# Two empty tiles of 32 and 128 bytes that move SBUF addresses in a float32 decoder-layer kernel

## The chip, the core and the metric

The kernel runs on one core of one Trainium2 chip. The metric is the device time of one execution in microseconds: the median of three executions, 1381.23 us before the change (1381.03 to 1384.09). One further execution was recorded by the hardware profiler; it took 1381.79 us, of which 1380.0 us lie between the first and the last instruction.

## The reference: what is computed

One inference step of a single hybrid layer, for two request groups that share the weights: a prompt of 256 tokens and 8 sample requests of 4 tokens, 288 token columns in all. All tensors are float32. Cut to what matters:

```
h    = rmsnorm(x) * (1 + sc1) + sh1                 # adaLN: sh, sc, g = silu(c) @ w_ada + b_ada
proj = h @ w_in                                     # 2048 -> 4632 columns
mix  = concat[pool_mixer(u), ssd_mixer(z, xbc, dt)] @ w_out
x    = x + g1 * mix
h2   = rmsnorm(x) * (1 + sc2) + sh2
gate, val = split(h2 @ w_up)                        # 2048 -> 2 * 5504
x    = x + g2 * ((silu(causal_dwconv(gate)) * val) @ w_down)
y    = rmsnorm(x)
```

The outputs are y for both groups and the new pooling, convolution, SSM and FFN states.

## The kernel before, in words

Features lie on the 128 partitions and tokens on the free axis, so each activation is a list of tiles of 128 x 288 float32, 1,152 bytes on a partition. Weights come from memory as one stream of pieces of 128 x 1024 float32 (`load`, into tiles `raw`), in the order in which they are used.

Every product of weights and features is made of three TensorE matmuls (`mm3`, lines 247 to 252). Both operands are split into a rounded high part and a remainder in the fp32r format, and the small-times-small product is left out. ScalarE writes the high part of a weight piece (`whi`, line 238), VectorE the remainder (`wlo`, line 240). The high and low parts of the features are the tiles `h1h`/`h1l`, `mixh`/`mixl`, `h2h`/`h2l` (made by `new_operand`) and `ah`/`al`. In a product the weights are the operand that is loaded into the array (LDWEIGHTS, 128 columns) and the features are the operand that streams past them (288 columns):

```
        nc.tensor.matmul(ps, whi[:, w], bh, start=first, stop=False)   # L250
        nc.tensor.matmul(ps, whi[:, w], bl, start=False, stop=False)   # L251
        nc.tensor.matmul(ps, wlo[:, w], bh, start=False, stop=last)    # L252
```

The stages follow each other: `xbc` and `mm_dt` (first input projection, with the adaLN products `adag` between), `mm_uz` (the rest of the input projection, with the SSD mixer between), `mm_out`, `mm_up`, then `mm_gate` and `mm_val` in turn for each of 40 column tiles of the FFN, with `mm_down` in three blocks. A projection of 16 feature tiles is 48 of these matmuls.

Where things lie in SBUF is set by pools. Pool `kp` lives through the kernel and grows from the low addresses; `mx`, `w0` and `sx` lie above it in the first half, and `ff` and `w2` take their place in the second half. Pool `w1` lies at the high end, from the right, and does not depend on the others. There are two sets of split weight slots: the two `whi` and two `wlo` slots of `w1`, used from the start, and two and two more in `w2`, added at line 1062 when `mm_out` has reached its sixth tile (m = 5). From then on pieces take the four slots in turn, so that in the FFN each `mm_gate` projection (two pieces) reads the slots of `w2`, each `mm_val` projection those of `w1`, and `mm_down` half from each. Counted over the program, 5,400 of the 8,736 matmuls of `mm3` read slots of `w1` and 3,336 read slots of `w2`.

A scheduler orders the instructions from their dependencies; the early part is kept in the order written.

Of the kernel before, what the change touches and what calls it, by code (L numbers as in the profile page):

```python
# [11 lines left out]
F32 = mybir.dt.float32  # L12
# [5 lines left out]
P = 128  # L18
# [119 lines left out]
def kernel(ctx: ExitStack, tc, ins, outs):  # L138
# [4 lines left out]
    kp = ctx.enter_context(tc.tile_pool(name="kp", bufs=1))  # L143
    pm = ctx.enter_context(tc.tile_pool(name="pm", bufs=3, space=PSUM))
    px = ctx.enter_context(tc.tile_pool(name="px", bufs=4, space=PSUM))
    pa = ctx.enter_context(tc.tile_pool(name="pa", bufs=1, space=PSUM))

    def aux(name):
        return px.tile([P, 512], F32, tag="aux", name=name)
# [49 lines left out]
    def new_operand(name):  # L199
        xhi[0] = [kp.tile([P, N], F32R, tag="xhi", name=f"{name}h{k}", bufs=KT) for k in range(KT)]  # L200
        xlo[0] = [kp.tile([P, N], F32R, tag="xlo", name=f"{name}l{k}", bufs=KT) for k in range(KT)]
# [263 lines left out]
    ups = mx.tile([P, 4, NB, 19], F32, name="ups")  # L465
    nc.vector.memset(upp[:, :, 0:15], 0.0)

    new_operand("h1")

    selr = mx.tile([P, 32], F32R, name="selr")  # L470
# [541 lines left out]
    mx_ctx.close()  # L1012
    ff = ctx.enter_context(tc.tile_pool(name="ff", bufs=1, reuse_waits="tile"))
    w2 = ctx.enter_context(tc.tile_pool(name="w2", bufs=1, reuse_waits="tile"))
    x = ff.tile([P, KT, N], F32, name="x")


# [340 lines left out]
```

## Time and profile before

| | |
|---|---|
| median of three executions | 1381.23 us |
| profiled execution | 1381.79 us, span 1380.0 us |
| TensorE matmuls (PE) | 99% of the span, 10,569 instructions |
| TensorE weight loads (PEld) | 91% |
| VectorE (DVE) | 60% |
| ScalarE (ACT) | 41% |
| GpSimd (POOL) | 16% |
| DMA queue of the weight stream | 62.5% of 16 engines |

In the views, PE rows are matmuls and PEld rows are weight loads, which run beside the matmul before them. A matmul's listed duration holds its latency and overlaps the next one, so the pace of TensorE is read from the distance between the starts of neighbouring matmuls and not from the listed duration. Names stand as out<-in by the program's tiles.

### The profile page before, as it was taken

The numbers are of one execution on the slowest core, as the hardware profiler recorded it, in microseconds if no ns is written. First come the engines' busy times: TensorE is split into PE (matmuls) and PEld (weight loads), VectorE is DVE, ScalarE is ACT, GpSimd is POOL, SyncE is SP. The second block draws the span as 40 slices with busy tenths as digits, with TensorE's granted clock in tenths as the row PEclk, the third lists the DMA queues.
The fourth block names the chain that finished last, engine by engine and source line by source line (L and its number), as shares of the span: only waits on it lengthen the run. The fifth ranks groups of instructions, "written<-read, shape, count | busy, mean of one in ns | idle before, by whom it ended". The sixth has DMA issues, their size and how long they took to land.

```text
span 1380.0 us, 26263 instructions
## 1 busy us (share of the span) xinstructions
PE 1360.7 (99%) x10569; PEld 1260.0 (91%) x10569; DVE 822.8 (60%) x1376; ACT 570.1 (41%) x889; POOL 224.4 (16%) x430
## 2 busy tenths in 40 slices
PE   8999999999999999999999999999999999999997
PEld 7888987776779899989999999999999999999997
DVE  5776557877574448654655445656565555566553
ACT  4223233478553335533433333443433334443452
POOL 0000001212122213111221001212120012122221
PEclk9999999999999999999999999999999999999998
DMA  9987756888887868687555455555554555555531
GB/s 380 408 355 296 281 215 258 328 297 297 306 338 294 317 244 284 231 278 290 189 176 181 171 167 185 202 184 184 187 172 162 184 196 180 195 190 190 185 119 70
DMA packets 97194, 323.20 MB, mean 234 GB/s; under 512 B 10736, under 2 KB 19888, under 8 KB 97072
## 3 DMA queue, kind: packets, MB, share of 16 engines
q1 hardware_dynamic: 93168, 310.63, 62.5%
q0 software_dynamic: 3184, 9.69, 1.8%
q8 instruction: 83, 1.36, 0.4%
q10 hardware_dynamic: 720, 1.19, 0.2%
q14 instruction: 39, 0.32, 0.1%
HBM read 309.78 MB, written 10.39 MB: 232 GB/s over the span
## 4 chain that ended last, share of the span: by engine, by line
PE 94%; DVE 4%; ACT 1%; issue 1%; POOL 0%; DMA 0%; DVEq 0%; POOLq 0%; ACTq 0%
PE mm_down L250 7%; PE mm_down L252 7%; PE mm_down L251 7%; PE mm_gate L250 6%; PE mm_val L251 6%; PE mm_val L252 6%; PE mm_val L250 6%; PE mm_gate L252 6%; PE mm_gate L251 6%; PE adap L279 4%; PE xbc L252 4%; PE xbc L250 4%; PE xbc L251 4%; PE mm_out L250 3%; PE mm_out L251 3%; PE mm_out L252 2%
## 5 line engine op out<-in xcount | busy, mean ns | idle before, releaser
L250 PE MATMUL mm_down<-ah,whi_down 128*128 128x288 f32 x688 | 203.8, 296 | 0.0
L252 PE MATMUL mm_down<-ah,wlo_down 128*128 128x288 f32 x688 | 203.6, 296 | 0.0
L251 PE MATMUL mm_down<-al,whi_down 128*128 128x288 f32 x688 | 203.4, 296 | 0.0
L251 PE MATMUL mm_val<-h2l,whi_val 128*128 128x288 f32 x640 | 191.3, 299 | 0.0
L252 PE MATMUL mm_val<-h2h,wlo_val 128*128 128x288 f32 x640 | 190.0, 297 | 0.0
L250 PE MATMUL mm_gate<-h2h,whi_gate 128*128 128x288 f32 x640 | 189.9, 297 | 0.0
L250 PE MATMUL mm_val<-h2h,whi_val 128*128 128x288 f32 x640 | 189.0, 295 | 0.0
L251 PE MATMUL mm_gate<-h2l,whi_gate 128*128 128x288 f32 x640 | 188.9, 295 | 0.0
L252 PE MATMUL mm_gate<-h2h,wlo_gate 128*128 128x288 f32 x640 | 188.7, 295 | 0.0
L240 DVE TENSOR_TENSOR wlo_gate<-raw_gate,whi_gate 128x1024 fp32r<-128x1024 f32 x80 | 97.9, 1225 | 138.6 <-ACT whi_gate L238 136.5
L240 DVE TENSOR_TENSOR wlo_down<-raw_down,whi_down 128x1024 fp32r<-128x1024 f32 x96 | 108.2, 1127 | 116.7 <-ACT whi_down L238 115.9
L238 ACT CAST whi_down<-raw_down 128x1024 fp32r<-128x1024 f32 x96 | 92.2, 960 | 169.2 <-PE mm_down L251 122.0
L238 ACT CAST whi_gate<-raw_gate 128x1024 fp32r<-128x1024 f32 x80 | 83.8, 1050 | 162.8 <-PE mm_gate L251 70.5
L250 PE MATMUL xbc<-h1h,whi_xbc 128*128 128x288 f32 x448 | 136.3, 306 | 1.7 <-ACT cvp L593 0.9
L238 ACT CAST whi_val<-raw_val 128x1024 fp32r<-128x1024 f32 x80 | 84.0, 1050 | 128.1 <-issue 102.2
L252 PE MATMUL xbc<-h1h,wlo_xbc 128*128 128x288 f32 x448 | 132.1, 302 | 2.6 <-DVE wlo_xbc L240 2.5
L251 PE MATMUL xbc<-h1l,whi_xbc 128*128 128x288 f32 x448 | 132.8, 297 | 0.0
L251 PEld LDWEIGHTS mm_down<-al,whi_down 128*128 128x128 f32 x688 | 129.8, 189 | 0.0
L252 PEld LDWEIGHTS mm_down<-ah,wlo_down 128*128 128x128 f32 x688 | 129.7, 189 | 0.0
L250 PEld LDWEIGHTS mm_down<-ah,whi_down 128*128 128x128 f32 x688 | 129.7, 188 | 0.0
L250 PEld LDWEIGHTS mm_gate<-h2h,whi_gate 128*128 128x128 f32 x640 | 120.1, 188 | 5.0 <-ACT ah L1123 3.4
L250 PEld LDWEIGHTS mm_val<-h2h,whi_val 128*128 128x128 f32 x640 | 120.9, 189 | 0.0
(322 smaller groups left out, 2992.9 us busy)
## 6 DMA issues: line engine op xcount, KB each, us to landing
raw_adap<-wflat SPq DMA_DIRECT2D x128, 512.0 KB, 5.5
raw_gate<-wflat SPq DMA_DIRECT2D x80, 512.0 KB, 3.5
raw_val<-wflat SPq DMA_DIRECT2D x80, 512.0 KB, 3.5
raw_ada<-wflat SPq DMA_DIRECT2D x64, 512.0 KB, 9.4
raw_xbc<-wflat SPq DMA_DIRECT2D x55, 512.0 KB, 7.2
raw_down<-wflat SPq DMA_DIRECT2D x48, 512.0 KB, 3.5
raw_out<-wflat SPq DMA_DIRECT2D x32, 512.0 KB, 6.9
raw_down<-wflat SPq DMA_DIRECT2D x32, 384.0 KB, 2.9
```

The costliest lines, as they stand in the source:

```text
L238: yield nc.scalar.copy(hi[:, :n], raw[:, a:a + n])
L240: nc.vector.tensor_tensor(lo[:, :n], raw[:, a:a + n], hi[:, :n].bitcast(F32), ALU.subtract)
L250: nc.tensor.matmul(ps, whi[:, w], bh, start=first, stop=False)
L251: nc.tensor.matmul(ps, whi[:, w], bl, start=False, stop=False)
L252: nc.tensor.matmul(ps, wlo[:, w], bh, start=False, stop=last)
L279: nc.tensor.matmul(ps[32 * j:32 * j + 32, :nb], sc_c[:, k, :], raw[:, c:c + nb], start=(k == 0), stop=(k == KT - 1), tile_position=(0, 32 ...
```

## The change

Two tiles that nothing writes or reads are allocated: one of 32 bytes on each partition in `kp`, just ahead of the first call of `new_operand`, and one of 128 bytes at the bottom of `w2`.

```
+    def shift(pool, nbytes):
+        pool.tile([P, nbytes // 4], F32, name="shift")
...
     nc.vector.memset(upp[:, :, 0:15], 0.0)
+    shift(kp, 32)
     new_operand("h1")
...
     w2 = ctx.enter_context(tc.tile_pool(name="w2", bufs=1, reuse_waits="tile"))
+    shift(w2, 128)
     x = ff.tile([P, KT, N], F32, name="x")
```

On all engines and in the DMA queues the built program has the same instructions in the same order with the same waits as before. What differs is addresses. Everything that is allocated in `kp` after the first tile, and all of `mx`, `w0`, `sx` and `ff`, lies 32 bytes higher; the tiles of `w2` lie 160 bytes higher (32 + 128); `w1` stays. Byte addresses on a partition:

| tiles | before | now | remainder by 128 before | now |
|---|---|---|---|---|
| `h1h`, `mixh`, `h2h` (16 tiles, 1,152 apart) | 22,656 and on | 22,688 and on | 0 | 32 |
| `h1l`, `mixl`, `h2l` | 41,088 and on | 41,120 and on | 0 | 32 |
| `ah` (17 tiles) | 108,032 and on | 108,064 and on | 0 | 32 |
| `al` (17 tiles) | 127,616 and on | 127,648 and on | 0 | 32 |
| `whi` slots of `w2` | 147,200 and 151,296 | 147,360 and 151,456 | 0 | 32 |
| `wlo` slots of `w2` | 155,392 and 159,488 | 155,552 and 159,648 | 0 | 32 |
| `raw` slot of `w2` | 163,584 | 163,744 | 0 | 32 |
| `whi` slots of `w1` | 212,960 and 217,056 | the same | 96 | 96 |
| `wlo` slots of `w1` | 221,152 and 225,248 | the same | 96 | 96 |

Inside a slot the weights of one matmul lie 512 bytes after those of the one before. Feature tiles that are used one after the other are 1,152 bytes apart, which is 128 more or less by a remainder of 256, so their remainder by 256 changes by 128 from one feature tile to the next.

More of the change, by code (lines that the diff above doesn't have):

```diff
@@ L146, with shift @@
     pa = ctx.enter_context(tc.tile_pool(name="pa", bufs=1, space=PSUM))
+    def shift(pool, nbytes):
+        pool.tile([P, nbytes // 4], F32, name="shift")
     def aux(name):
@@ L466 @@
     nc.vector.memset(upp[:, :, 0:15], 0.0)
+    shift(kp, 32)
     new_operand("h1")
@@ L1014 @@
     w2 = ctx.enter_context(tc.tile_pool(name="w2", bufs=1, reuse_waits="tile"))
+    shift(w2, 128)
     x = ff.tile([P, KT, N], F32, name="x")
```

## The prediction

> **What bounds the kernel now.** I read the page's busy shares, then the chain of waits, then busy times by stage, then single matmuls.
>
> ```profile
> span 1380.0 us, 26263 instructions
> PE 1360.7 (99%) x10569; PEld 1260.0 (91%) x10569; DVE 822.8 (60%) x1376; ACT 570.1 (41%) x889; POOL 224.4 (16%) x430
> PE 94%; DVE 4%; ACT 1%; issue 1%; POOL 0%; DMA 0%; DVEq 0%; POOLq 0%; ACTq 0%
> ```
>
> ```profile
> core 0: us, PE busy (x) PEld busy (x) DVE busy (x) ACT busy (x) POOL busy (x), PEclk, DMA share, GB/s
> 0.00:200.00 200.00, 193.55 (x1792) 169.68 (x1793) 128.10 (x240) 63.94 (x89) 5.96 (x16) 1.00 0.86 331
> 200.00:400.00 200.00, 196.68 (x1512) 144.56 (x1510) 149.49 (x312) 122.62 (x247) 41.02 (x68) 0.99 0.78 289
> 650.00:1366.00 716.00, 716.00 (x5363) 716.00 (x5362) 403.06 (x587) 283.25 (x400) 125.63 (x253) 1.00 0.52 176
> ```
>
> The chain that ended last is 94% TensorE. From 650 to 1366 us nothing makes TensorE wait: 716.00 of 716.00 us busy, DMA at half load, clock granted in full. There 5,363 matmuls take 716 us, 133.5 ns apart on average, nearly all of them 128x288 products. The time of this stage is therefore a number of matmuls times a pace, and only the pace can move it. The first 400 us have 9.8 us of TensorE idle time, so a faster pace is worth a little less there.
>
> **Does the pace depend on where the operands lie?** The change alters no instruction, so this is the question. The trace holds a natural comparison: mm_gate and mm_val have the same shapes and the same feature tiles, in turns, in one stage. They differ in the set of weight slots: mm_gate reads w2, whose slots lie at remainder 0 by 128 like the feature tiles; mm_val reads w1, at remainder 96.
>
> ```profile
> L251 PE MATMUL mm_val<-h2l,whi_val 128*128 128x288 f32 x640 | 191.3, 299 | 0.0
> L252 PE MATMUL mm_val<-h2h,wlo_val 128*128 128x288 f32 x640 | 190.0, 297 | 0.0
> L250 PE MATMUL mm_val<-h2h,whi_val 128*128 128x288 f32 x640 | 189.0, 295 | 0.0
> L250 PE MATMUL mm_gate<-h2h,whi_gate 128*128 128x288 f32 x640 | 189.9, 297 | 0.0
> L251 PE MATMUL mm_gate<-h2l,whi_gate 128*128 128x288 f32 x640 | 188.9, 295 | 0.0
> L252 PE MATMUL mm_gate<-h2h,wlo_gate 128*128 128x288 f32 x640 | 188.7, 295 | 0.0
> ```
>
> The three lines of mm_val list 299, 297 and 295 ns, those of mm_gate 297, 295 and 295. The starts of three projections in a row, 48 matmuls each, say it as pace:
>
> ```profile
> 914.28 0.29 PE L250 MATMUL mm_gate<-h2h,whi_gate 128*128 128x288 f32 x1
> ...
> 920.67 0.29 PE L250 MATMUL mm_val<-h2h,whi_val 128*128 128x288 f32 x1
> ...
> 927.10 0.29 PE L250 MATMUL mm_gate<-h2h,whi_gate 128*128 128x288 f32 x1
> ```
>
> mm_gate takes 6.39 us, which is 133.1 ns a matmul; mm_val takes 6.43 us, 134.0 ns. The difference is 0.04 us in 48, or 0.83 ns a matmul. Inside mm_val it is not even:
>
> ```profile
> 912.05 0.30 PE L251 MATMUL mm_val<-h2l,whi_val 128*128 128x288 f32 x1
> ...
> 912.45 0.30 PE L251 MATMUL mm_val<-h2l,whi_val 128*128 128x288 f32 x1
> ...
> 912.86 0.30 PE L251 MATMUL mm_val<-h2l,whi_val 128*128 128x288 f32 x1
> ...
> 913.26 0.30 PE L251 MATMUL mm_val<-h2l,whi_val 128*128 128x288 f32 x1
> ```
>
> One feature tile (three matmuls) takes 0.40 us, the next 0.41, the next 0.40. The feature tiles alternate by 128 in their remainder by 256 while the slots do not, so I read this as: weight reads and feature reads get in each other's way by a few ns, depending on the distance of their addresses. No wait is listed at these matmuls. This reading is an inference; nothing in the trace shows a memory bank.
>
> **The change, part by part.**
>
> *The 32 bytes, for the w1 products (5,400 of 8,736).* Features go from remainder 0 to 32 by 128 and the w1 slots stay at 96. The distance from features to weights goes from 96 or 224 by 256 (the fast and the slow half above) to 64 or 192. No matmul of before has that distance with ordinary weights, so I bound it from both sides. The nearest row for a gain that stays within one stage is mm_gate: if w1 products run at the w2 pace, 5,400 x 0.83 ns = 4.5 us are won, of which the 1,344 xbc products (1.1 us) lie in the first 200 us and are partly lost in waits: 3.4 to 4.5 us. A farther row has the very distance that comes: cse streams csr, which lies at byte 127,520, remainder 32 by 128, while either one repeated column or the w1 weights of mm_uz are loaded.
>
> ```profile
> 275.84 0.43 PE L740 MATMUL cse<-csr,selr 128*128 128x288 f32 x2
> 276.10 0.29 PE L250 MATMUL mm_uz<-h1h,whi_uz 128*128 128x288 f32 x1
> ...
> 277.70 0.43 PE L740 MATMUL cse<-csr,selr 128*128 128x288 f32 x2
> 277.96 0.29 PE L250 MATMUL mm_uz<-h1h,whi_uz 128*128 128x288 f32 x1
> ```
>
> Two matmuls take 0.26 us from start to start, 130 ns each with 5 ns of rounding; I use 131. Against 134.0 that is 3.0 ns, and 5,400 x 3.0 = 16 us. This is the far end for a gain, because those matmuls stand alone among others and load one repeated column half the time. They also say that a feature operand at an odd multiple of 32 bytes costs nothing by itself. The end for a loss is the slow feature tile of mm_val, 0.41 / 3 = 136.7 ns, in every w1 product: 2.7 ns x 5,400 = +14.6 us. Between -16 and +14.6 I take a little more than the nearest row, **-5 us**: the slow half has a distance that goes away, and the one sample of the new distance is fast.
>
> *The 128 bytes, for the w2 products (3,336).* Features and w2 slots both move to remainder 32 by 128, so their distance stays 0 or 128 by 256. With 160 bytes for one and 32 for the other, the feature tiles that had the one distance get the other. Each half of the tiles has either, so I take **0**; the bound is the spread between slot sets, 0.83 ns x 3,336 = 2.8 us either way.
>
> *Other engines and the DMAs.* They read and write moved tiles as well. Splitting shows no price of place, at w1 (val) or w2 (gate):
>
> ```profile
> L238 ACT CAST whi_val<-raw_val 128x1024 fp32r<-128x1024 f32 x80 | 84.0, 1050 | 128.1 <-issue 102.2
> L238 ACT CAST whi_gate<-raw_gate 128x1024 fp32r<-128x1024 f32 x80 | 83.8, 1050 | 162.8 <-PE mm_gate L251 70.5
> L240 DVE TENSOR_TENSOR wlo_gate<-raw_gate,whi_gate 128x1024 fp32r<-128x1024 f32 x80 | 97.9, 1225 | 138.6 <-ACT whi_gate L238 136.5
> raw_gate<-wflat SPq DMA_DIRECT2D x80, 512.0 KB, 3.5
> raw_val<-wflat SPq DMA_DIRECT2D x80, 512.0 KB, 3.5
> ```
>
> ScalarE takes 1050 ns for both. VectorE and ScalarE wait for work (136.5 us on ScalarE's result, 70.5 us for a free slot), and loads land in 3.5 us where a projection lasts 6.4, so even 1% on each would stay hidden behind TensorE after 400 us. I take **0**. If that cover were gone, in the first 200 us at 0.86 DMA share, 1% of slower loads would be at most 2 us.
>
> *Sum.* -5 + 0 + 0 on the profiled 1381.8 us gives 1376.8; the profiled execution lies 0.6 us above the median shown, so on the median's scale it is **1376.2 us**, -0.36%. What a measurement of this kernel tells from no change is about 0.3%, or 4.1 us: 0.77 ns on each w1 product. The forecast stands just beyond that.
>
> **The rivals.**
>
> *The place doesn't matter enough: 1381 us.* The alternation averages out: the new distances 64 and 192 are again one fast and one slow half. For it: distances 0 and 128 (mm_gate) and 96 and 224 (mm_val) differ by only 0.83 ns on average. Against it: the slow half exists at all. A rule speaks for this rival. The Trainium skill, "TensorE: Matmul & The Clock Gate", Part 2, says that TensorE has two independent SBUF read ports and that loading the next weights takes no read bandwidth from the running matmul. "SBUF — State Buffer", Door 1, gives lines of 16 bytes, of which 32 and 128 are whole multiples. By both the time would stay at 1381; the 0.40 and 0.41 us in turn do not agree with a full independence.
>
> *The new distance is the bad one: slower.* The mechanism is the one above at the same place, the 5,400 w1 products: both 64 and 192 lie in the slow state that mm_val has on every other feature tile. Fully locked it costs +14.6 us, 1396; half of it, +7, gives 1388. It decides the sign from 0.77 ns a product on. For it: only one of the four known distances is clearly slow, and nothing says how wide that region is. Against it: cse at 131.
>
> *A deep gain: 1365 us.* All w1 products run at the pace of cse, -16 us. For it: the same row. Against: cse never runs in a long row with full weights.
>
> **How the numbers follow.** Forecast (mild gain, its own range 1371 to 1379) 0.42, of which 0.10 lies within 0.3%; deep gain 0.12; no change 0.25; slower 0.21. So faster 0.44, same 0.35, slower 0.21. The range reaches down to 1364, just past the deep gain, and up to 1391, the slow rival's middle and some more; beyond it lies the fully locked case, about 0.1, and some 0.05 below.
>
> **What would show it.** Between 650 and 1366 us the same 5,363 matmuls should take some 3 us less, with PE still busy throughout. A mm_val projection should fall from 6.43 to 6.39 us or below, without the turn of 0.40 and 0.41; a mm_gate projection should stay at 6.39. ACT 1050 ns and DVE 1225 ns should not move. I am wrong in size if mm_val drops under 6.35 or if mm_gate moves as well; wrong in sign if mm_val rises to 6.5; wrong in mechanism if the time moves and the pace of these two does not, or if it is the first 400 us that move.

## The result, and the profile after

The changed kernel takes 1374.32 us (median of five executions, 1373.55 to 1375.51) where the kernel before took 1381.23 us in the same comparison: a ratio of 0.9948 with a 95% interval of 0.9933 to 0.9962, or 6.9 us less. The profiled execution took 1375.51 us with a span of 1373.7 us, 6.3 us under the 1380.0 us of before. One execution below, the profiled one of e4, ran at a granted clock of 0.751 and took 1635 us, where the other five of that kernel have 0.995 to 0.997; it is left out of e4's median and ratio.

The page of the changed kernel, its busy shares and its chain of waits:

```profile
span 1373.7 us, 26263 instructions
PE 1353.4 (99%) x10569; PEld 1252.7 (91%) x10569; DVE 822.1 (60%) x1376; ACT 569.9 (41%) x889; POOL 224.9 (16%) x430
PE 94%; DVE 4%; DMA 1%; issue 0%; ACT 0%; POOL 0%; SPq 0%; DVEq 0%; POOLq 0%; ACTq 0%
```

TensorE is busy 7.3 us less, the other engines do what they did, and the chain is TensorE's as before. Where the time went is seen when both executions are cut at the same instructions: the start of mm_out, of mm_up, of the first mm_gate, and the last mm_down. First the kernel before, then the changed one; the columns are the stretch, its length, busy time and number of instructions of each engine, the clock, the DMA share and GB/s.

```profile
0.00:391.50 391.50, 383.68 (x3269) 310.69 (x3269) 269.13 (x529) 181.60 (x326) 45.79 (x82) 1.00 0.82 310
391.50:522.50 131.00, 129.05 (x954) 110.96 (x950) 62.08 (x108) 46.12 (x66) 26.79 (x41) 1.00 0.80 303
522.50:561.00 38.50, 38.50 (x291) 38.38 (x289) 32.63 (x58) 21.08 (x37) 12.15 (x19) 1.00 0.77 268
561.00:1366.60 805.60, 805.60 (x6035) 796.57 (x6034) 452.03 (x665) 320.07 (x458) 139.63 (x289) 1.00 0.54 186
```

```profile
0.00:390.60 390.60, 381.77 (x3269) 308.75 (x3269) 269.06 (x529) 181.50 (x326) 45.85 (x82) 1.00 0.82 310
390.60:520.90 130.30, 128.31 (x954) 110.18 (x950) 62.08 (x108) 46.21 (x66) 26.98 (x41) 1.00 0.81 305
520.90:559.30 38.40, 38.40 (x291) 38.30 (x289) 32.49 (x58) 20.99 (x37) 12.16 (x19) 1.00 0.77 261
559.30:1360.30 801.00, 801.00 (x6035) 791.99 (x6034) 451.60 (x665) 319.95 (x458) 139.88 (x289) 1.00 0.56 187
```

Each stretch has the same number of matmuls in both. The FFN gives 4.6 us (805.60 to 801.00, TensorE busy throughout), the first 390 us 0.9, mm_out 0.7, mm_up 0.1. In the first stretch TensorE is busy 1.9 us less and the stretch is only 0.9 us shorter: half of the gain there is lost in waits.

The groups of mm_gate and mm_val in the changed kernel, whose lines are numbered 5 higher:

```profile
L255 PE MATMUL mm_gate<-h2h,whi_gate 128*128 128x288 f32 x640 | 190.0, 297 | 0.0
L256 PE MATMUL mm_gate<-h2l,whi_gate 128*128 128x288 f32 x640 | 189.1, 295 | 0.0
L256 PE MATMUL mm_val<-h2l,whi_val 128*128 128x288 f32 x640 | 189.0, 295 | 0.0
L257 PE MATMUL mm_val<-h2h,wlo_val 128*128 128x288 f32 x640 | 188.8, 295 | 0.0
L257 PE MATMUL mm_gate<-h2h,wlo_gate 128*128 128x288 f32 x640 | 188.4, 294 | 0.0
L255 PE MATMUL mm_val<-h2h,whi_val 128*128 128x288 f32 x640 | 188.2, 294 | 0.0
```

mm_val went from 295, 299 and 297 ns to 294, 295 and 295; mm_gate stayed. The starts of the same three projections that the prediction shows (the 20th of the 40 pairs of mm_gate and mm_val, and the mm_gate behind it), and of three feature tiles inside mm_val, in the changed kernel:

```profile
910.35 0.29 PE L255 MATMUL mm_gate<-h2h,whi_gate 128*128 128x288 f32 x1
...
916.74 0.29 PE L255 MATMUL mm_val<-h2h,whi_val 128*128 128x288 f32 x1
...
923.09 0.29 PE L255 MATMUL mm_gate<-h2h,whi_gate 128*128 128x288 f32 x1
```

```profile
919.92 0.29 PE L255 MATMUL mm_val<-h2h,whi_val 128*128 128x288 f32 x1
...
920.31 0.29 PE L255 MATMUL mm_val<-h2h,whi_val 128*128 128x288 f32 x1
...
920.71 0.29 PE L255 MATMUL mm_val<-h2h,whi_val 128*128 128x288 f32 x1
```

mm_gate takes 6.39 us as before, mm_val 6.35 instead of 6.43. The turn of 0.40 and 0.41 us is gone, and what is left is 0.39 and 0.40. Averaged over the 40 mm_val projections, a feature tile of the slow half takes 396.2 ns after 405.3, and one of the fast half 397.7 after 399.2: most of the gain comes from the slow half, and the fast half gained a little too. Averaged over all w1 products that follow each other directly, the three matmuls of a feature tile take 396.9 ns after 401.0; those of w2 take 399.0 after 399.2.

### The profile page after: what moved, and what is told of

Read it like the earlier page. It is cut to its first block, busy times and chain, and to the rows that moved or that the text cites. A ratio compares the mean times of both kernels' runs of the same rounds, so it can differ in the third digit from the quotient of the medians.

```text
span 1373.7 us, 26263 instructions
## 1 busy us (share of the span) xinstructions
PE 1353.4 (99%) x10569; PEld 1252.7 (91%) x10569; DVE 822.1 (60%) x1376; ACT 569.9 (41%) x889; POOL 224.9 (16%) x430
## 4 chain that ended last, share of the span: by engine, by line
PE 94%; DVE 4%; DMA 1%; issue 0%; ACT 0%; POOL 0%; SPq 0%; DVEq 0%; POOLq 0%; ACTq 0%
PE mm_down L255 7%; PE mm_down L256 7%; PE mm_down L257 7%; PE mm_gate L255 6%; PE mm_val L256 6%; PE mm_gate L257 6%; PE mm_gate L256 6%; PE mm_val L257 6%; PE mm_val L255 6%; PE adap L284 4%; PE xbc L257 4%; PE xbc L255 4%; PE xbc L256 4%; PE mm_out L255 3%; PE mm_out L256 3%; PE mm_out L257 2%
## 5 line engine op out<-in xcount | busy, mean ns | idle before, releaser
L243 ACT CAST whi_gate<-raw_gate 128x1024 fp32r<-128x1024 f32 x80 | 83.7, 1048 | 161.9 <-PE mm_gate L256 70.5
L243 ACT CAST whi_val<-raw_val 128x1024 fp32r<-128x1024 f32 x80 | 84.1, 1051 | 125.0 <-issue 100.1
L256 PE MATMUL xbc<-h1l,whi_xbc 128*128 128x288 f32 x448 | 132.2, 296 | 0.0
```

The costliest lines, as they stand in the source:

```text
L243: yield nc.scalar.copy(hi[:, :n], raw[:, a:a + n])
```

## The experiments

The theory under test: the pace of a product follows the distance, by 256, from the streamed features to the weights that are being loaded beside them. The rivals: the features' own place, the slots' own place, or something else than the weight stream. Three starts, those of the 20th mm_gate, its mm_val and the next mm_gate, give the pace in each run. All runs, with the ratio to the kernel before in the same comparison and its interval:

| run | distances w1 | w2 | mm_gate us | mm_val us | time us | ratio |
|---|---|---|---|---|---|---|
| before | 96, 224 | 0, 128 | 6.39 | 6.43 | 1381.2 | |
| the change | 64, 192 | 0, 128 | 6.39 | 6.35 | 1374.3 | 0.9948 [0.9933, 0.9962] |
| e1 32 bytes alone | 64, 192 | 0, 128 | 6.39 | 6.35 | 1376.1 | 0.9960 [0.9947, 0.9974] |
| e2 128 bytes alone | 96, 224 | 0, 128 | 6.38 | 6.40 | 1379.3 | 0.9985 [0.9976, 0.9995] |
| e3 w1 slots 32 lower | 64, 192 | 0, 128 | 6.40 | 6.35 | 1373.9 | 0.9953 [0.9939, 0.9967] |
| e4 32 and 64 bytes | 64, 192 | 64, 192 | | | 1372.4 | 0.9937 [0.9925, 0.9949] |
| e5 64 bytes in kp | 32, 160 | 0, 128 | 6.40 | 6.35 | 1376.4 | 0.9966 [0.9952, 0.9979] |
| e6 96 bytes in kp | 0, 128 | 0, 128 | 6.40 | 6.39 | 1376.7 | 0.9967 [0.9956, 0.9978] |
| e7 distance restored | 96, 224 | 0, 128 | 6.39 | 6.42 | 1380.9 | 1.0002 [0.9993, 1.0011] |
| e8 as e4 | 64, 192 | 64, 192 | 6.34 | 6.35 | 1371.2 | 0.9932 [0.9918, 0.9945] |
| e9 one column, old places | | | 6.33 | 6.35 | 1372.1 | 0.9934 [0.9918, 0.9951] |
| e10 one column, new places | | | 6.33 | 6.35 | 1370.6 | 0.9922 [0.9907, 0.9937] |
| e11 96 bytes, low parts 128 on | 0, 128 | 0, 128 | 6.39 | 6.41 | 1374.1 | 0.9947 [0.9932, 0.9962] |
| e12 as e8, low parts 128 on | 64, 192 | 64, 192 | 6.35 | 6.35 | 1372.8 | 0.9935 [0.9920, 0.9949] |

The intervals are wide beside the differences: by time alone e1, e5 and e6 cannot be told from each other. The paces in the traces tell them apart.

### e1: the 32 bytes alone

```
+    shift(kp, 32)
     new_operand("h1")
```

> The 32-byte tile alone. Distance theory (the pace of a product follows the distance, by 256, from the streamed features to the weights being loaded): w1 products have the changed kernel's distances 64 and 192, so a mm_val projection takes 6.35 us as there and mm_gate 6.39 to 6.40 us; time 1374 to 1375 us, all of the gain. Rival (the 128 bytes carry part of it, through the w2 slots): 1376 to 1378 us, with mm_gate slower than 6.40.

```profile
910.46 0.30 PE L253 MATMUL mm_gate<-h2h,whi_gate 128*128 128x288 f32 x1
...
916.85 0.30 PE L253 MATMUL mm_val<-h2h,whi_val 128*128 128x288 f32 x1
...
923.20 0.29 PE L253 MATMUL mm_gate<-h2h,whi_gate 128*128 128x288 f32 x1
```

Measured: 1376.1 us, and paces that cannot be told from those of the change: mm_gate 6.39 us, mm_val 6.35, a span of 1373.8 us against 1373.7. The median misses the theory's 1374 to 1375 and lies inside the rival's 1376 to 1378, but the rival wanted mm_gate over 6.40, and it is not. The intervals of the two ratios overlap, so the time alone does not separate them. The 32 bytes carry all of the gain that can be seen in the trace.

### e2: the 128 bytes alone

```
+    shift(w2, 128)
     x = ff.tile([P, KT, N], F32, name="x")
```

> The 128-byte tile alone: features stay at remainder 0 and w2 slots go to 128, so each product keeps its pair of distances (0 and 128 for w2, 96 and 224 for w1). Distance theory: no change, mm_val 6.43 us, mm_gate 6.39, time 1381 us within 1.5. Rival (the 128 bytes matter by themselves): 2 us or more away from 1381.

```profile
913.69 0.29 PE L253 MATMUL mm_gate<-h2h,whi_gate 128*128 128x288 f32 x1
...
920.07 0.30 PE L253 MATMUL mm_val<-h2h,whi_val 128*128 128x288 f32 x1
...
926.47 0.29 PE L253 MATMUL mm_gate<-h2h,whi_gate 128*128 128x288 f32 x1
```

A miss for the theory in its strict form. The time is 1379.3 us, 0.9985 with an interval that leaves out 1, and mm_val takes 6.40 us instead of 6.43, with w1 slots and features exactly where they were before. Within mm_val the slow and the fast feature tiles have changed places: on average 395 ns for the tiles at distance 224 and 405 for those at 96, where the kernel before has 405 and 399. What differs is only the place of the w2 slots, which mm_gate reads just ahead. So the same distances can run in more than one rhythm (a steady pattern of fast and slow feature tiles). That the products ahead decide which is a guess at this point; e11 bears on it.

### e3: the other side moved

```
-    wp[0].add(ctx.enter_context(tc.tile_pool(name="w1", bufs=1, side="right")), RAW1, SPLIT1)
+    w1 = ctx.enter_context(tc.tile_pool(name="w1", bufs=1, side="right"))
+    wp[0].add(w1, RAW1, SPLIT1)
...
+    shift(w1, 32)
     mx_ctx.close()
```

All tiles of w1, its `raw` slots too, lie 32 bytes lower; nothing else moves.

> Features stay where they were (remainder 0 by 128), and the slots of w1 go 32 bytes down instead, from remainder 96 to 64. The distance of w1 products is 64 or 192, as in the changed kernel. Distance theory: mm_val 6.35 us, time 1374 to 1375. Rival (what counts is the place of the features themselves, remainder 32 being good): mm_val stays at 6.43, time 1381. Second rival (the slots' own place): no theory for the size, mm_val anywhere but 6.35.

```profile
908.44 0.30 PE L253 MATMUL mm_gate<-h2h,whi_gate 128*128 128x288 f32 x1
...
914.84 0.30 PE L253 MATMUL mm_val<-h2h,whi_val 128*128 128x288 f32 x1
...
921.19 0.29 PE L253 MATMUL mm_gate<-h2h,whi_gate 128*128 128x288 f32 x1
```

mm_val takes 6.35 us and the kernel 1373.9 us, with every feature tile at its old place. The features' own place is ruled out as the cause: the gain comes whichever side moves, with the same distance.

### e4 and e8: the w2 slots at the good distance too

```
+    shift(kp, 32)
     new_operand("h1")
...
+    shift(w2, 64)
     x = ff.tile([P, KT, N], F32, name="x")
```

> 32 bytes in kp and 64 instead of 128 in w2: now the w2 products have the distances 64 and 192 too. Distance theory: mm_gate falls from 6.40 to the 6.35 us of mm_val; 3,336 products at 0.7 ns less are 2.3 us, time 1372 us. Rival (w1 and w2 differ for another reason than the distance): mm_gate stays at 6.40, time 1374.5.

The time is 1372.4 us, close to the 1372 of the theory. The trace kept of it cannot be set beside the others, so e8 is the same kernel once more.

> The kernel with all products at the distances 64 and 192 once more, for an undisturbed trace. Distance theory: mm_gate 6.35 us like mm_val, and a time near 1372. Rival: mm_gate 6.40, 1374.5.

```profile
907.54 0.29 PE L253 MATMUL mm_gate<-h2h,whi_gate 128*128 128x288 f32 x1
...
913.88 0.29 PE L253 MATMUL mm_val<-h2h,whi_val 128*128 128x288 f32 x1
...
920.23 0.29 PE L253 MATMUL mm_gate<-h2h,whi_gate 128*128 128x288 f32 x1
```

mm_gate falls to 6.34 us, as its distance said it would: at the same distances the two slot sets run within 0.01 us. At 1371.2 us this has the lowest time of the kernels here that compute the whole reference; e12, at 1372.8, is too close to be told from it. It is well clear of the kernel before (0.9932). It lies 3.1 us under the changed kernel in medians from different comparisons; the intervals of the two ratios overlap slightly, but the 40 mm_gate projections at 0.05 us less give 2.0 us of it in the trace.

### e5 and e6: the other two pairs of distances

```
+    shift(kp, 64)        # e6: shift(kp, 96)
     new_operand("h1")
```

> 64 bytes in kp alone: w1 products get the distances 32 and 160, the last pair that multiples of 32 allow; w2 products keep 0 and 128. Distance theory: mm_gate as before, 6.39 to 6.40 us; mm_val has a pace of its own, between the pairs known so far, 6.35 to 6.43 us; time 1374 to 1381. Rival (any move of the features off remainder 0 wins): 6.35 and 1374.

```profile
909.52 0.30 PE L253 MATMUL mm_gate<-h2h,whi_gate 128*128 128x288 f32 x1
...
915.92 0.30 PE L253 MATMUL mm_val<-h2h,whi_val 128*128 128x288 f32 x1
...
922.27 0.30 PE L253 MATMUL mm_gate<-h2h,whi_gate 128*128 128x288 f32 x1
```

mm_val takes 6.35 us, at the low end of what was expected, so 32 and 160 are as good there as 64 and 192. Not so in mm_down: on w1 slots it takes 399.8 ns for three matmuls after 399.5 before and gained nothing, where the change brought it to 396.5. The time is 1376.4 us, which cannot be told from e1's 1376.1.

> 96 bytes in kp alone: features at remainder 96 like the w1 slots, so w1 and w2 products both have the distances 0 and 128. Distance theory: mm_val runs like mm_gate, 6.39 to 6.40 us instead of 6.43 before; 5,400 products at 0.6 ns less are 3.4 us, time 1378 us. Rival (any move of the features wins): 1374.

```profile
913.01 0.29 PE L253 MATMUL mm_gate<-h2h,whi_gate 128*128 128x288 f32 x1
...
919.41 0.29 PE L253 MATMUL mm_val<-h2h,whi_val 128*128 128x288 f32 x1
...
925.80 0.29 PE L253 MATMUL mm_gate<-h2h,whi_gate 128*128 128x288 f32 x1
```

With the distances of mm_gate, mm_val takes mm_gate's time, 6.39 us. This rules out that any move of the features wins. The time is 1376.7, 1.3 us under the expected 1378. In the trace mm_down on w1 slots fell to 393.3 ns for three matmuls, faster than in any other run, while on w2 slots at the same distances it took 398.2. The theory has no account of that.

### e7: the changed kernel with the old distance

```
+    shift(kp, 32)
...
+    shift(w2, 128)
...
+    shift(w1, 96)
     mx_ctx.close()
```

The last of them puts all tiles of w1 96 bytes lower.

> The changed kernel with the w1 slots 96 bytes lower, at remainder 0: features stay at remainder 32 and w2 slots at 32, but the w1 products have the old distances 96 and 224 again. Distance theory: the gain is gone, mm_val 6.40 to 6.43 us, time 1379 to 1381. Rival (the features' own place): 1374, mm_val 6.35.

```profile
913.20 0.29 PE L253 MATMUL mm_gate<-h2h,whi_gate 128*128 128x288 f32 x1
...
919.59 0.30 PE L253 MATMUL mm_val<-h2h,whi_val 128*128 128x288 f32 x1
...
926.01 0.29 PE L253 MATMUL mm_gate<-h2h,whi_gate 128*128 128x288 f32 x1
```

The gain is gone: 1.0002, mm_val 6.42 us, although features and w2 slots lie where the change put them. Together with e3 this shows that the gain follows the distance between the features and the tiles of w1. The `raw` slots of w1 moved along in e3 and e7, so the traffic of other engines there could still be the partner; that is what e9 tests.

### e9 and e10: no weight stream

```
-        w = slice(c * n, c * n + n)
-        nc.tensor.matmul(ps, whi[:, w], bh, start=first, stop=False)
+        one = slice(c * n, c * n + 1)
+        h1, l1 = whi[:, one].to_broadcast([P, n]), wlo[:, one].to_broadcast([P, n])
+        nc.tensor.matmul(ps, h1, bh, start=first, stop=False)
...
```

The other two matmuls of `mm3` are changed alike.

> The kernel before, at its old addresses, but each weight load repeats the first of its 128 columns (the other 127 columns of every weight block are left out of the computation). The loads last as many columns but read one place instead of 512 bytes in a row. Distance theory (the partner of the feature stream is the weight stream): mm_val and mm_gate run alike and faster than before, near the 131 to 132 ns of cse, 6.30 to 6.35 us, without a turn of fast and slow feature tiles. Rival (the partner is something else, as another engine's traffic): mm_val 6.43, mm_gate 6.39 as before.

```profile
907.67 0.29 PE L254 MATMUL mm_gate<-h2h,whi_gate 128*128 128x288 f32 x1
...
914.00 0.29 PE L254 MATMUL mm_val<-h2h,whi_val 128*128 128x288 f32 x1
...
920.35 0.29 PE L254 MATMUL mm_gate<-h2h,whi_gate 128*128 128x288 f32 x1
```

> The same cut (one column repeated) in the changed kernel, with the 32 and 128 bytes. Distance theory: no weight stream, so the 7 us between the two layouts are gone: within 2 us of the kernel at the old addresses. Rival: 7 us faster than it.

```profile
906.05 0.29 PE L254 MATMUL mm_gate<-h2h,whi_gate 128*128 128x288 f32 x1
...
912.38 0.29 PE L254 MATMUL mm_val<-h2h,whi_val 128*128 128x288 f32 x1
...
918.73 0.29 PE L254 MATMUL mm_gate<-h2h,whi_gate 128*128 128x288 f32 x1
```

At the old places mm_val falls from 6.43 to 6.35 us without any move, every feature tile of it takes the same 397 ns, and mm_gate falls to 6.33 (6.35 in the median of the 40). Of the 6.9 us between the two layouts 1.5 are left (1372.1 and 1370.6, intervals overlapping). The DMAs, ScalarE and VectorE still fill the same slots, so the partner of the feature stream is the reading of the 512 bytes of weights. About 132 ns a matmul remain when the weights are one place, and the layout of e8, with all its weights, runs at that pace too. It is not a floor: 4 of the 80 projections of e10 take 6.24 to 6.25 us, 130 ns a matmul (the mm_gate that starts at 1097.99 us and its mm_val, at 1104.24, are two of them). So a faster rhythm exists without a weight stream, too. In these two kernels mm_down keeps a turn of its own, 400 and 398 ns for three matmuls in both layouts and on both slot sets, which a stream of weights cannot cause; what does is open.

### e11 and e12: high and low parts in opposite halves

```
         xhi[0] = [kp.tile([P, N], F32R, tag="xhi", ...) for k in range(KT)]
+        if xlo[0] is None:
+            kp.tile([P, 32], F32, name="between")
         xlo[0] = [kp.tile([P, N], F32R, tag="xlo", ...) for k in range(KT)]
```

e11 has this with 96 bytes in kp, e12 with 32 bytes in kp and 64 in w2. So far the tiles `h2h` and `h2l` of one number had the same remainder by 256, while `ah` and `al` of mm_down differ by 128.

> 96 bytes in kp and 128 more between the high and the low feature parts, so that in every product, as so far only in mm_down, high and low parts lie 128 apart by 256; all weights at distances 0 and 128. In the kernel with 96 bytes mm_down ran at 131.1 ns on w1 slots and 132.7 on w2 slots. If the opposite halves of high and low part make that: all products near 131 to 132, 1364 to 1370 us. If it was a state that mm_down fell into by its own sequence: mm_val and mm_gate stay at 6.39, time 1375 to 1378.

Neither case as written. The 17th pair of projections, then the 20th, of this kernel:

```profile
871.61 0.29 PE L255 MATMUL mm_gate<-h2h,whi_gate 128*128 128x288 f32 x1
...
877.85 0.29 PE L255 MATMUL mm_val<-h2h,whi_val 128*128 128x288 f32 x1
...
884.09 0.29 PE L255 MATMUL mm_gate<-h2h,whi_gate 128*128 128x288 f32 x1
```

```profile
909.40 0.29 PE L255 MATMUL mm_gate<-h2h,whi_gate 128*128 128x288 f32 x1
...
915.79 0.29 PE L255 MATMUL mm_val<-h2h,whi_val 128*128 128x288 f32 x1
...
922.20 0.29 PE L255 MATMUL mm_gate<-h2h,whi_gate 128*128 128x288 f32 x1
```

Both pairs read the same slots and the same features, and one takes 6.24 us a projection and the other 6.39 and 6.41. Of the 80 projections 18 run at 6.24, whole projections at a time and two to six in a row; the rest take 6.39 to 6.40 (the first ones, beside the `adap` matmuls, up to 6.49). That is what e2 had hinted at: the addresses allow several rhythms. The pace never changes where one projection follows another directly. All five stretches of 6.24 begin at a mm_gate behind two `hs` matmuls (the state update of the SSD mixer), and the four that end before the last projection end at a mm_gate behind `hs` or mm_down. So the start of a projection decides, and the rhythm is handed on to the next; most starts behind `hs` stay slow, and what makes the difference is not shown. The time is 1374.1 us.

> The fastest layout so far (all weights at distances 64 and 192 from the features, 1371.2 us) with 128 bytes more between high and low feature parts, which in the run with 96 bytes let some projections run at 6.24 us where others of the same addresses took 6.40. If the paces follow the distances alone: mm_gate and mm_val stay at 6.34 to 6.35 and the time at 1371 within 2 us. If opposite halves open a second, faster rhythm here too: a part of the projections at 6.24 us, 1363 to 1369 us. If they open a slower one: 6.40 and 1374 to 1376.

Measured 1372.8 us, and no projection at 6.24: 6.34 to 6.35 but for the first ones, beside the `adap` matmuls, as the distances alone say.

## Why the prediction was right

**What bounds the kernel** was read correctly. TensorE is busy through the FFN in both kernels, the number of matmuls is the same, and 4.6 of the 6.3 us of span came there. The matmuls that lay between 650 and 1366 us take 4.0 us less, where the forecast was some 3.

**The first term, the w1 products, had the right sign, place and mechanism and was too small:** -5 us was taken, and 1.4 ns a product (401.0 to 396.9 ns for three) on 5,400 products are 7.4 us, of which about 1 was lost in early waits, as the prediction had it for the xbc products. The step that was mis-sized is the choice of the nearest row: mm_gate's pace was taken as what a good distance gives, with a little added. e9 shows that mm_gate's distances 0 and 128 are not free either. Without the weight stream the pace is about 132 ns, mm_gate runs at 133.1 and mm_val ran at 134.0. The far row, cse, which had the coming distance, was the better witness: its 0.26 us for two matmuls, read as 131 ns, was within rounding of 132, and over the 13 cse matmuls that the next one follows at once the trace has 132. Used at 132 it would have given 2.0 x 5,400 = 11 us, still too much: the w1 products stood at 133.7 on average, not at mm_val's 134.0, and came to 132.3. The bound for a loss was too wide: the slow feature tile, read as 0.41 us from rounded starts, takes 405.3 ns, or 135.1 a matmul, and 1.1 x 5,400 is +6 us in place of +14.6. That the forecast came within 2 us is partly luck: between bounds of -16 and +14.6 it leaned on a row of another distance, and the sign on a few cse matmuls.

**That the slow half of the feature tiles goes away** was right: 405.3 to 396.2 ns. The fast half, for which the working has no gain, gained 1.5 ns too. mm_val stopped at 6.35 us, just at the mark below which the prediction called itself wrong in size.

**The second term, 0 for the w2 slots,** held. mm_gate stayed at 6.39, and the 32 bytes alone leave the same paces. The 128 bytes do matter where the w1 products are at their old distance (e2, 2 us), which the prediction did not see.

**The 0 for other engines and DMAs** held: splits take 1048 and 1051 ns on ScalarE after 1050, and loads land in 3.6 and 3.8 us, still well inside a projection.

**The rivals.** "The place doesn't matter enough" falls with e3 and e7. The rule of the Trainium skill that stood behind it ("TensorE: Matmul & The Clock Gate", Part 2: two independent read ports, no read bandwidth taken) does not hold here to the last per cent: before against e9 is 134.0 against 132.2 ns in mm_val for the same number of matmuls and weight loads. The slow rival was wrong about the distance: 64 and 192 have the lowest average over the w1 products of the four pairs, 396.9 ns for three, with 32 and 160 next at 397.5 (e5). The deep gain at 131 ns did not come from the change, though e10 and e11 show 130 ns (6.24 us for 48) to be possible.

**What stays open:** what in the memory meets, what starts a rhythm, and why mm_down on w1 slots is fastest at 0 and 128 (e6), against the order of the other stages. The period of 256 bytes is read from the turn of slow and fast feature tiles, 1,152 bytes apart; no run moves a tile by 256 to test it. None of the runs looks below the pace.

## What to carry to other kernels

When TensorE runs matmul after matmul without a wait, the pace itself can depend on addresses: look at starts of neighbouring matmuls by weight buffer, and if two buffers with the same work differ, try an empty tile of 32 to 96 bytes ahead of one. Here the distance from streamed operand to weights is worth 0.5 to 0.7% of the time, and 64 bytes off a multiple of 128, for every weight buffer, is the layout that reached the pace without any weight stream. Judge such a move by the pace per projection in the trace rather than by a time that scatters by 0.2%: inside one execution mm_val repeats to some 10 ns in 6.4 us once the `adap` matmuls are done, except in the two layouts with a second rhythm (e10, e11). Look at all projections, then, and not at one.

## What the runs showed of the hardware that was not expected

- The same instructions at the same addresses have more than one steady rhythm: 6.24 or 6.40 us for 48 matmuls in e11, 6.24 or 6.35 in e10, where the weights are one place. A rhythm lasts for a whole projection and goes on in the next one that follows directly. With w1 slots and features in place, moving only the w2 slots changed the rhythm of mm_val: 399 and 405 ns a feature tile before, 405 and 395 in e2 (distances 96 and 224).
- Without a weight stream a 288-column fp32r matmul still takes about 132 ns here, and at best 130 was seen over a projection (e10, e11). The Trainium skill's "TensorE: Matmul & The Clock Gate", Back-to-back issue gap, has N / 2.4 + 2.5 ns for a matmul by itself, an estimate of 122.5 ns for 288 columns, and says that in a stream of weight loads and matmuls both set the spacing. No projection of any run came near 122.5.
- Lines of 16 bytes ("SBUF — State Buffer", Door 1, in the Trainium skill) cannot be all that matters: moves by whole lines take mm_val from 6.43 to 6.35 us (32 bytes, e1 and e3) and back to 6.42 (96 bytes more, e7).
